# The convolution's output product in seven products instead of eight, with weight sums made by accumulating transfers

## The chip, the core and the metric

The kernel runs on one core of a Trainium2 chip. The metric is the device time of one execution in microseconds (us). The engines are PE (matrix products), DVE (elementwise, also called VectorE), ACT (activations and copies), POOL (here almost only the issuing of transfers, among them those that add to their destination) and SP (the issuing of transfers). Each engine takes its instructions in the order in which they were recorded; semaphores order the engines among each other.

## The reference

The model is a trunk of two layers in float32 on 1024 positions of width 1024: a gated short convolution, a SwiGLU FFN, dilated attention, a second FFN, with an RMSNorm before each and one at the end. What the change touches is the convolution mixer and the norm behind it:

```
def short_conv_mixer(h, w_in, conv_k, w_out):
    b, c, u = jnp.split(h @ w_in, 3, axis=-1)
    y = depthwise_causal_conv(c * u, conv_k)     # width 3
    return (b * y) @ w_out
...
h = rms_norm(x, mix_norm[0]);  x = x + short_conv_mixer(h, ...)
h = rms_norm(x, ffn_norm[0]);  x = x + (silu(h @ w_gate) * (h @ w_up)) @ w_down
```

## The kernel before

Everything is held transposed: `X[n]` is a page of 128 channels by 1024 positions, n = 0 to 7, and the positions are worked on in two halves of 512. Float32 products are made of three matmuls: each operand is split into a high part (a copy on ACT, rounded to the matmul's format) and a low part (a subtraction on DVE), and hi·hi, hi·lo and lo·hi are summed in a PSUM bank. So each weight tile costs one ACT and one DVE instruction (`split`, L157 and L158), and so does each operand tile (`hi`, L604 and L605).

Most large products use a seven-product scheme for 2 by 2 blocks (class `Strassen`): weights in rows and contraction halves, activations in contraction halves and position halves. The seven products are numbered 1 to 7; 3, 5, 6 and 7 take sums of weight blocks and sums of activation blocks. Sums of weights are made on DVE (`combo`, L225). The sums of activations for an FFN's down product are made when a quad of blocks is complete (`store`, L784), and go to DRAM as `part`; `feed` brings them back (`hin`), splits them and hands them to `down`, which runs the products in the order of `DOWN`: 1, 2, 6, 7, 4, 5, 3.

The convolution's output product was the exception. `Conv.store` put each block y to DRAM as `plain_conv`; `first_tiles` and `group1` multiplied whole tiles: first channels 0 to 3 for all eight n and both halves (`first_tiles`, added to a loaded X), then channels 4 to 7, the first position half for all n, and then the second half (`by_columns`, called by `group1`). After each addition into X, `chained` squares it (ACT) for the next norm and POOL or DVE adds the squares; at the end of the first half the statistics are summed over channels by PE with a matrix of ones, and `first_half` makes the FFN's first operands one by one: `scaled` (DVE, tile hcol), its high part (ACT), then the previous one's low part (DVE). `gained` follows on ACT for each n whose second half is complete.

The order on each engine is the order in which this Python code records; there is no planner. `ensure` and `take` decide how far ahead weights are split. `bias_tables` makes the attention's bias tables in three pieces, placed at three points of the first FFN's down product by `after`.

## Time and profile before

| | us |
|---|---|
| median of 3 runs | 2089.16 (2088.01 to 2090.88) |
| profiled execution | 2087.8 |
| its span, first to last instruction | 2086.0 |
| PE busy | 2069.0 (99%) |
| DVE busy | 1760.0 (84%) |
| ACT busy | 1027.9 (49%) |
| POOL busy | 269.8 (13%) |

The convolution's input products run until 242.2 us, its output product from 242.22 to 329.76, where the FFN's first product begins. The profile's page gives a matmul's busy time from start to modelled end; in the order of time one sees when each starts. Idle time of an engine is put down to what ended it.

### The profile page before, as it was taken

How to read it: one execution, taken by the hardware profiler on the slowest of the kernel's cores; microseconds unless marked ns; L12 is line 12 of the kernel's file. 1: busy time of each engine (PE TensorE's matmuls, PEld its weight loads, DVE VectorE, ACT ScalarE, POOL GpSimd, SP SyncE). 2: the span in 40 equal slices, each digit the busy share in tenths (PEclk: the TensorE clock that was granted, in tenths of full speed). 3: DMA queues.
4: the chain of work that ended last, by engine and by line, in shares of the span. 5: the costliest groups of instructions: out<-in, count | busy, mean ns of one | idle time of the engine just before them, and what ended most of it. 6: DMA issues, size and time to landing. Idle time of an engine off the chain costs nothing.

```text
span 2086.0 us, 30813 instructions
## 1 busy us (share of the span) xinstructions
PE 2069.0 (99%) x10954; PEld 1784.5 (86%) x10954; DVE 1760.0 (84%) x3302; ACT 1027.9 (49%) x1902; POOL 269.8 (13%) x381
## 2 busy tenths in 40 slices
PE   9999999999999999999999999999999999999998
PEld 7788888888888888878889999998888888888887
DVE  8898769988888889798985888987998888887896
ACT  8333427444444455355544666665544444455443
POOL 1000000110100111010223333211001011002000
PEclk9999999999999999999999999999999999999999
DMA  7332643233233477443657867855222333368532
GB/s 222 96 96 71 237 131 76 102 106 111 102 107 101 159 247 209 161 127 128 227 187 207 210 173 219 240 186 143 76 91 101 106 107 106 115 204 228 162 101 81
DMA packets 133929, 305.70 MB, mean 147 GB/s; under 512 B 15580, under 2 KB 46382, under 8 KB 133776
## 3 DMA queue, kind: packets, MB, share of 16 engines
q1 hardware_dynamic: 96128, 203.51, 32.2%
q0 software_dynamic: 30016, 85.52, 13.5%
q10 hardware_dynamic: 7632, 14.70, 1.9%
q8 instruction: 87, 1.43, 0.3%
q14 instruction: 66, 0.54, 0.1%
HBM read 209.99 MB, written 84.50 MB: 141 GB/s over the span
## 4 chain that ended last, share of the span: by engine, by line
PE 94%; DVE 3%; ACT 1%; issue 0%; DMA 0%; DVEq 0%; ACTq 0%
PE bank L612 21%; PE bank L614 21%; PE bank L613 21%; PE bank L1714 5%; PE bank L415 3%; PE bank L416 3%; PE bank L417 3%; PE bank L707 3%; PE bank L704 3%; PE bank L706 3%; PE bank L1583 2%; PE bank L1585 1%; PE bank L1584 1%; PE bank L1640 1%; PE bank L1639 1%; DVE b L605 0%
## 5 line engine op out<-in xcount | busy, mean ns | idle before, releaser
L612 PE MATMUL bank<-b,w 128*128 128x512 f32 x2064 | 804.4, 390 | 3.0 <-ACT w L157 1.6
L614 PE MATMUL bank<-b,w 128*128 128x512 f32 x2064 | 804.0, 390 | 3.1 <-DVE w L158 3.0
L613 PE MATMUL bank<-b,w 128*128 128x512 f32 x2064 | 804.1, 390 | 0.6 <-DVE b L924 0.6
L614 PEld LDWEIGHTS bank<-b,w 128*128 128x128 f32 x2064 | 387.5, 188 | 86.9 <-DVE w L158 6.1
L612 PEld LDWEIGHTS bank<-b,w 128*128 128x128 f32 x2064 | 387.7, 188 | 83.1 <-ACT w L157 2.0
L613 PEld LDWEIGHTS bank<-b,w 128*128 128x128 f32 x2064 | 387.7, 188 | 79.7 <-DVE b L924 1.4
L157 ACT ACTIVATE w<-combo 128x512 fp32r<-128x512 f32 (+2 forms) x496 | 259.0, 549 | 266.7 <-DVE combo L225 227.9
L158 DVE TENSOR_TENSOR w<-combo,w 128x512 fp32r<-128x512 f32 (+2 forms) x496 | 286.2, 590 | 33.0 <-ACT w L157 32.7
L618 ACT ACTIVATE part<-bank 128x512 f32<-128x512 f32 x192 | 114.4, 596 | 394.0 <-PE bank L614 390.6
L158 DVE TENSOR_TENSOR w<-raw,w 128x512 fp32r<-128x512 f32 (+2 forms) x340 | 190.4, 581 | 36.8 <-ACT w L157 36.6
L622 DVE TENSOR_TENSOR part<-part,bank 128x256 f32<-128x256 f32 (+1 forms) x372 | 174.8, 498 | 34.8 <-PE bank L614 18.6
L157 ACT ACTIVATE w<-raw 128x512 fp32r<-128x512 f32 (+2 forms) x340 | 171.3, 537 | 27.4 <-PE bank L707 10.5
L415 PE MATMUL bank<-w_hi,w 128*128 128x512 f32 (+1 forms) x336 | 126.3, 376 | 0.0
L416 PE MATMUL bank<-w_lo,w 128*128 128x512 f32 (+1 forms) x336 | 124.2, 370 | 0.0
L417 PE MATMUL bank<-w_hi,w 128*128 128x512 f32 (+1 forms) x336 | 124.2, 370 | 0.0
L839 DVE TENSOR_TENSOR x<-x,bank 128x512 f32<-128x512 f32 x136 | 92.8, 683 | 30.0 <-PE bank L614 29.1
L225 DVE TENSOR_TENSOR combo<-raw 128x512 f32<-128x512 f32 (+1 forms) x176 | 116.0, 659 | 0.0
L605 DVE TENSOR_TENSOR b<-hin,b 128x512 fp32r<-128x512 f32 x140 | 95.2, 685 | 15.6 <-ACT b L604 15.5
L534 DVE TENSOR_TENSOR x<-x,bank 128x512 f32<-128x512 f32 (+1 forms) x88 | 55.7, 635 | 41.3 <-PE bank L417 40.6
L604 ACT ACTIVATE b<-hin 128x512 fp32r<-128x512 f32 x140 | 86.0, 619 | 5.1 <-DMA hin<-part 3.6
L707 PE MATMUL bank<-b,w 128*128 128x256 f32 x288 | 81.5, 283 | 0.0
L706 PE MATMUL bank<-b,w 128*128 128x256 f32 x288 | 81.5, 283 | 0.0
(233 smaller groups left out, 3318.5 us busy)
## 6 DMA issues: line engine op xcount, KB each, us to landing
hin<-part SPq DMA_DIRECT2D x140, 256.0 KB, 4.4
raw<-in_ffn_w_gate SPq DMA_DIRECT2D x44, 512.0 KB, 3.6
raw<-in_ffn_w_up SPq DMA_DIRECT2D x44, 512.0 KB, 3.6
part<-sum POOLq DMA_DIRECT2D x80, 256.0 KB, 2.3
raw<-in_attn_w_qkv SPq DMA_DIRECT2D x27, 512.0 KB, 4.5
raw<-in_conv_w_in SPq DMA_DIRECT2D x24, 512.0 KB, 4.2
raw<-in_ffn_w_down SPq DMA_DIRECT2D x32, 384.0 KB, 5.3
part<-part POOLq DMA_DIRECT2D x40, 256.0 KB, 2.5
```

The costliest lines, as they stand in the source:

```text
L157: nc.scalar.activation(hi, src, AF.Copy)
L158: low = lambda: eng.tensor_tensor(out=lo, in0=src, in1=hi, op=ALU.subtract)
L225: eng.tensor_tensor(out=c, in0=a, in1=b, op=op)
L415: nc.tensor.matmul(b, whi[:, a], ahi[:, s], start=first, stop=False)
L416: nc.tensor.matmul(b, whi[:, a], alo[:, s], start=False, stop=False)
L417: nc.tensor.matmul(b, wlo[:, a], ahi[:, s], start=False, stop=last)
L612: nc.tensor.matmul(b, hi[:, a], bhi, start=start and k == 0, stop=False, skip_group_check=True)
L613: nc.tensor.matmul(b, hi[:, a], blo, start=False, stop=False, skip_group_check=True)
L614: nc.tensor.matmul(b, lo[:, a], bhi, start=False, stop=k == n - 1, skip_group_check=True)
L622: nc.vector.tensor_tensor(out=t, in0=t, in1=b, op=ALU.add)
L706: nc.tensor.matmul(b, hi[:, a], blo, start=False, stop=False, skip_group_check=True)
L707: nc.tensor.matmul(b, lo[:, a], bhi, start=False, stop=k == n - 1, skip_group_check=True)
```

## The change

The output product joins the seven-product scheme (`CONV_PAIRS, CONV_CHUNK = 4, 4`: all eight channel tiles in one chunk of four pairs). `first_tiles`, `halved` and `below` go; `down` serves the convolution too, with four units of two n each for the seven products. `store` makes four differences for each of the four quads, and signs are chosen such that the weights are only added: the banks of odd n hold the negated result and are subtracted from X[n] instead of added.

- `add_summed` replaces DVE's sums of weights: two pages for each unit, a and b, are loaded; after a block has been split, an accumulating transfer on POOL adds the next weight block to it in the page. The FFN's weights keep DVE's sums (`add_pair`), with the sign turned.
- `ensure` loads these pages ahead by `LEAD = 4` weights. The conv's operands are read one tile ahead (`feed(1)`), the first four during the last unit's products 7, 4 and 3 (`CONV_FEED`).
- X starts with ACT's copy of a bank; the source is added by an accumulating transfer on POOL (after products 1, 6 and 7), or loaded by SP and added to.
- `entry` replaces `group1` ahead of the first FFN: squares, spills and the first half's operands follow products 2, 4, 5 and 3. The first half of the even n is complete with product 2, of the odd n with product 4, the second half with products 5 and 3. `first_half` makes the odd tiles 1, 3, 5, 7 first and then 0, 2, 4, 6, each together with `gained`.
- `bias_tables` runs later, at three points of the down product's last chunk: (0,7,2), (0,4,4), (0,5,4) instead of (-1,3,2), (0,1,2), (0,2,0).

```diff
+    def add_summed(u, ab, cd, w):
...
+        def part(m):
+            p = t["a" if m in (1, 7, 6, 3) else "b"]
+            left, right = p[:, :w], p[:, w:2 * w]
+            out = split(left if m in (1, 2, 7) else right, None, nc.vector)
+            if m == 1:
+                accumulate(pair(p), twice(cd))
+            elif m == 2:
+                accumulate(t["a"][:, w:2 * w], block(cd, 1))
+            elif m == 6:
+                accumulate(right, block(ab, 1))
+            elif m == 4:
+                accumulate(right, block(cd, 0))
...
         def down(self, c, feed):
...
+                if fresh and not (one and (n % 2, h) == (1, 0)):
+                    nc.scalar.activation(X[n][:, half(h)], b, AF.Copy, scale=-1.0 if n % 2 else 1.0)
                 else:
-                    nc.vector.tensor_tensor(out=X[n][:, half(h)], in0=X[n][:, half(h)], in1=b, op=ALU.add)
+                    nc.vector.tensor_tensor(out=X[n][:, half(h)], in0=X[n][:, half(h)], in1=b,
+                                            op=ALU.subtract if n % 2 else ALU.add)
...
+        def entry(c, m, k):
+
+            j = k // 2
...
+            if m not in (2, 4, 5, 3):
+                return
+            n, h, at = k + (m in (4, 5)), int(m in (5, 3)), j + 4 * (m in (4, 3))
+            norm.chained(at, *HALVES[h], 0, n)
+            nc.scalar.dma_start(spill[n][:, half(h)], X[n][:, half(h)])
...
+            elif (m, j) == (5, 1):
+                run(pre.pop())
+                pre.append(sw.first_half((1, 3, 5, 7, 0, 2, 4, 6)))
+            if m == 3:
+                ensure(first_op + 2 + j)
+            for t in {(5, 2): (1,), (5, 3): (3,), (3, 0): (5, 7), (3, 1): (0,), (3, 2): (2,), (3, 3): (4, 6)}.get((m, j), ()):
+                step(t)
...
-            if (c, m, k) in ((-1, 3, 2), (0, 1, 2), (0, 2, 0)):
+            if (c, m, k) in ((0, 7, 2), (0, 4, 4), (0, 5, 4)):
                 next(tab, None)
```

The change moves much of the order. The first place is DVE at the end of the output product. Before, the FFN's first product takes operands k = 0 to 3, and the last of their low parts (b_2819) stood among additions of the second half; x is a page of X, hcol a normed tile, acc the sum of squares:

```order
L605 TENSOR_TENSOR b_2813<-hcol_2811,b_2813 128x512
L534 TENSOR_TENSOR x_2310<-x_2310,bank_2823 128x512
L1312 SCALAR_TENSOR_TENSOR hcol_2840<-x_2310,gains_68,rstd_2583 128x512
L605 TENSOR_TENSOR b_2819<-hcol_2817,b_2819 128x512
L534 TENSOR_TENSOR x_2345<-x_2345,bank_2847 128x512
```

Two more tiles of the output product followed on PE behind the bank of x_2345. Now k = 2 is the tile of x_2319, and its low part (b_3007) stands behind the addition of the output product's very last bank, 2889; w is a weight's pair of parts:

```order
L160 TENSOR_TENSOR w_3002<-raw_2736,w_3002 128x512
L1336 SCALAR_TENSOR_TENSOR hcol_3005<-x_2319,gains_68,rstd_2422 128x512
L649 TENSOR_TENSOR b_2980<-hcol_2978,b_2980 128x512
L896 TENSOR_TENSOR x_2388<-x_2388,bank_2889 128x512
L533 TENSOR_TENSOR acc_2421<-acc_2421,sq_2997 128x512
L160 TENSOR_TENSOR w_3028<-raw_2736,w_3028 128x512
L1336 SCALAR_TENSOR_TENSOR hcol_3031<-x_2349,gains_68,rstd_2422 128x512
L649 TENSOR_TENSOR b_3007<-hcol_3005,b_3007 128x512
```

The low part has moved from a place well ahead of the first product to one behind the last addition. The second place is POOL around the last quad. Before, its queue held the stores alone:

```order
L771 DMA plain_conv_6_165<-y_1883 128x512
L771 DMA plain_conv_7_166<-y_2105 128x512
L771 DMA plain_conv_7_166<-y_2048 128x512
L771 DMA plain_conv_6_165<-y_2185 128x512
L492 DMA acc_2582<-sq_2591 128x512
```

Now accumulations into the weight pages (summed) and into X stand between them; part_conv_3_2 is the last quad's tile for product 2:

```order
L843 DMA part_conv_3_1_180<-y_2028 128x512
L235 DMA summed_2075<-in_conv_w_out 128x2x512
L235 DMA summed_2096<-in_conv_w_out 128x2x512
L843 DMA part_conv_3_3_182<-y_2182 128x512
L235 DMA summed_2123<-in_conv_w_out 128x2x512
L235 DMA summed_2147<-in_conv_w_out 128x2x512
L235 DMA summed_2075<-in_conv_w_out 128x512
L886 DMA x_2286<-in_x 128x512
L235 DMA summed_2096<-in_conv_w_out 128x512
L886 DMA x_2319<-in_x 128x512
L843 DMA part_conv_3_2_181<-y_2120 128x512
```

The second transfer into summed_2096 follows the first into the same page, and the store of part_conv_3_2 has come to stand behind both.

More of the change, by code (lines that the diff above doesn't have):

```diff
@@ L216, in add_slab, with accumulate, load, add_pair @@
         ops.append((key, lambda: split(get_raw(i)[:, :width(src)])))
-    def add_pair(u, rows, w, eng, upto, low=()):
+    def add_summed(u, ab, cd, w):
+        t = {}
+        block = lambda src, h: view(src, h * w, [[1, w]])
+        twice = lambda src: view(src, 0, [[0, 2], [1, w]])
+        pair = lambda p: view(p, 0, [[w, 2], [1, w]])
+        rows = (cd.offset - ab.offset, 2)
+        def accumulate(dst, src):
+            nc.gpsimd.dma_start(out=dst, in_=src, accum_op=ALU.add)
+        def load(name):
+            t[name] = page("summed")
+            nc.sync.dma_start(pair(t[name]), twice(ab) if name == "a" else view(ab, w, [rows, [1, w]]))
+        def part(m):
[10 more added lines that the diff above has]
+                accumulate(right, block(cd, 0))
+            if m in (5, 3):
+                del t["a" if m == 3 else "b"]
+            return out
+        fetch_of["m", u, 1], fetch_of["m", u, 2] = lambda: load("a"), lambda: load("b")
+        return {m: (("m", u, m), lambda m=m: part(m)) for m in WINOGRAD}
+    def add_pair(u, rows, w, eng, upto, low=(), sub=ALU.subtract):
         t = {}
@@ L593, in __init__ @@
             self.st, self.quads, self.hid, self.deep = {}, {}, {}, {}
-            self.banks = set()
+            self.banks, self.there, self.after = set(), set(), None
+            self.lead = 1 if key == CONV else 2
             self.ahead, self.now = 2, 0
@@ L852, in down, with drain @@
                     add(n, h, b)
-                    if c == 0 and m in (2, 4, 5, 3):
-                        nc.gpsimd.dma_start(out=X[n][:, half(h)], in_=self.source[n][:, half(h)], accum_op=ALU.add)
+                    if c == 0 and m in ((1, 6, 7) if one else (2, 4, 5, 3)):
+                        source(n, h, nc.gpsimd, accum_op=ALU.add)
+                    if one and m == 1:
+                        X[n + 1] = page("x")
+                        source(n + 1, 0, nc.sync)
                     if m == 4:
                         del p[k]
+                    self.drain(c, m, k)
                     if k // 2 in steps:
                         next(feed, None)
-                    self.downed(c, m, k)
-        def downed(self, c, m, k):
+                    if self.after:
+                        self.after(c + 1 - len(self.chunks), m, k)
+        def drain(self, c, m, k):
             pass
@@ L889, in filled @@
                 if self.key == CONV:
-                    self.below(n, last)
+                    if self.order[n] in CONV_FEED:
+                        for _ in range(CONV_FEED[self.order[n]]):
+                            next(feed)
                 else:
@@ L1009, in conv @@
                     nc.vector.scalar_tensor_tensor(o, a, tap(i), o, op0=ALU.mult, op1=ALU.add)
-            eng = nc.vector
-            eng.tensor_tensor(out=y, in0=y, in1=self.norm.rstd[:, half(h)], op=ALU.mult)
+            nc.vector.tensor_tensor(out=y, in0=y, in1=self.norm.rstd[:, half(h)], op=ALU.mult)
             self.y[t, h] = y
@@ L1051, in idle, with drain, mix @@
                 self.step(2)
-        def halved(self, fs):
-            raw = {}
-            for f in list(fs) + [None]:
-                if f is not None:
-                    raw[f] = page("hin")
-                    nc.sync.dma_start(raw[f], self.plain[f])
-                for g in list(raw):
-                    if g != f:
-                        self.hid[g] = split(raw.pop(g))
-                yield
-        def below(self, n, last):
-            if self.order[n][0] == last and n >= self.at(last, 2) - self.base:
-                ensure(self.base + n + 2)
-                next(self.low, None)
-            if self.order[n] == (last, 7):
-                self.load_x(0, 1)
-                ensure(self.at(last, 3) + 2)
-        def first_tiles(self):
-            run(self.low)
-            upper = self.halved(range(CO, KT))
-            for n in range(KT):
-                banks = two_banks()
-                run(product(take(("co", 0, n), min(max(n - 2, 2), 4)), range(CO), self.hid, banks))
-                if n + 2 < KT:
-                    self.load_x(n + 2)
-                add_to_x(n, banks)
-                self.step(4 if n < 2 else None)
-                if n >= 3:
-                    next(upper, None)
-            run(upper)
-            for f in range(CO):
-                del self.plain[f]
+        def drain(self, c, m, k):
+            if self.waiting:
+                self.step(4 if (m, k) in ((1, 0), (1, 2)) else None)
         def out(self, u, c, v):
             self.waiting.append(self.work(u, c, v))
-        def mix(self, group1):
-            norm = self.norm
+        def mix(self, entry):
+            norm, self.after = self.norm, entry
             prep = self.operands()
@@ L1315, in scaled, with first_half @@
             return t
[L1317 removed]
+        def first_half(self, order=range(KT)):
             lo = None
[L1319 removed]
+            for k in order:
                 t = self.scaled(k, 0, half_page("hcol"))
```

121 lines of the change are left out of this document (69 added, 52 removed).

## The prediction

> **What bounds the kernel now.** I read the page first, then PE's waits, then the stage that is rewritten. The page says that one engine sets the time:
>
> ```profile
> span 2086.0 us, 30813 instructions
> PE 2069.0 (99%) x10954; PEld 1784.5 (86%) x10954; DVE 1760.0 (84%) x3302; ACT 1027.9 (49%) x1902; POOL 269.8 (13%) x381
> ```
>
> PE is busy for 2069.0 of 2086.0 us, so a matmul taken out is worth its time unless a new wait takes its place. PE's time per matmul must not be read from the page's mean of 390 ns: that is a matmul from start to modelled end, and successive ones overlap. The order of time of the convolution's output product shows the pitch:
>
> ```profile
> 242.22 0.39 PE L415 MATMUL bank<-w_hi,w 128*128 128x512 f32 x1
> ...
> 329.54 0.39 PE L417 MATMUL bank<-w_hi,w 128*128 128x512 f32 x1
> 329.76 0.39 PE L612 MATMUL bank<-b,w 128*128 128x512 f32 x1
> ```
>
> 384 matmuls and 2 small column sums lie between 242.22 and 329.76: 87.54 / 386 = 0.2268 us each. Now the stage by windows (columns: PE, PEld, DVE, ACT and POOL busy with their counts, granted clock, DMA share, GB/s), and the only wait of PE from 242 to 400 us:
>
> ```profile
> 104.00:156.00 52.00, 52.00 (x231) 43.08 (x230) 49.64 (x99) 19.77 (x35) 3.80 (x7) 1.00 0.31 97
> 242.00:286.00 44.00, 44.00 (x196) 36.44 (x195) 27.13 (x44) 11.52 (x17) 1.62 (x3) 1.00 0.53 181
> 317.00:330.00 13.00, 13.00 (x60) 10.74 (x59) 11.13 (x18) 10.34 (x18) 2.56 (x3) 1.00 0.51 114
> 330.00:360.00 30.00, 29.73 (x131) 24.30 (x130) 29.64 (x50) 20.75 (x36) 2.57 (x3) 1.00 0.30 74
> ```
> ```profile
> PE bank L528 <- DVE sum L520: 0.3, 1, 0.3
> ```
>
> The granted clock is 1.00 and PE never stands still, but the stage ends beside a VectorE that is almost full: 11.1 of 13 us, then 29.6 of 30. It stays ahead because all additions into the first half of X were done before the second half's products began, so the first half's norm could be worked on under them. That lead is what I look for in the changed order.
>
> **What the change takes off PE.** Seven products of 4 row units by 4 contraction tiles by 3 matmuls are 336 instead of 384: 48 x 0.2268 = **10.9 us**. (By the 0.39 mean it would be 18.7; the rows above exclude that.) The bias table's four matmuls now stand before a later product. Where they stood, the waits of PE over the whole run name two:
>
> ```profile
> PE bank L560 <- issue: 1.1, 1, 1.1
> PE bank L612 <- DVE t L562: 0.8, 1, 0.8
> ```
> ```profile
> 892.40 1.84 DVE L562 TENSOR_TENSOR t<-bank,low 16x512 f32<-16x512 f32 x4
> ```
>
> The first is the fourth of these matmuls, which finds no free bank because DVE is behind with its additions; the second is the product after them, which waits for DVE to read a bank. At the new place DVE has fewer additions before it, so I take off 1.9 us (bounds 0 and 1.9). Their vector work (the third row begins it) now ends nearer to query/key's first products; I add back a third of its 1.84, 0.6 (bounds 0 and 1.9).
>
> The conv stage gains four differences for each of four quads, 2.4 us of DVE and four stores on POOL a quad. Two of the quads fall about the fullest window, 104:156: DVE busy for 49.6 us there in 99 instructions, but each of them overlaps the next by 0.085 (0.685 from start to end, 0.60 from start to start, below), so some 41 of 52 us are taken, and 4.8 more fit. I cost these at nothing until the last quad; without that cover they would cost 4.8.
>
> **The seam into the FFN, on DVE and ACT.** Durations for it come from the old seam. First DVE, then ACT, in order of time:
>
> ```profile
> 316.18 0.75 DVE L1312 SCALAR_TENSOR_TENSOR hcol<-x,gains,rstd 128x512 f32<-128x512 f32 x1 [1.94 <-ACT rstd L530]
> 316.85 0.68 DVE L534 TENSOR_TENSOR x<-x,bank 128x512 f32<-128x512 f32 x1
> 318.76 0.69 DVE L158 TENSOR_TENSOR w<-raw,w 128x512 fp32r<-128x512 f32 x1 [1.24 <-ACT w L157]
> 319.37 0.75 DVE L1312 SCALAR_TENSOR_TENSOR hcol<-x,gains,rstd 128x512 f32<-128x512 f32 x1
> ...
> 321.95 0.69 DVE L158 TENSOR_TENSOR w<-raw,w 128x512 fp32r<-128x512 f32 x1 [0.64 <-ACT w L157]
> ...
> 340.99 2.49 DVE L1342 TENSOR_TENSOR x<-x,rstd 128x512 f32<-128x512 f32 x4
> ```
> ```profile
> 317.50 0.71 ACT L1334 ACTIVATE x<-x,less 128x512 f32<-128x512 f32 x1
> 318.12 0.62 ACT L157 ACTIVATE w<-raw 128x512 fp32r<-128x512 f32 x1
> 318.64 0.62 ACT L489 ACTIVATE sq<-x 128x512 f32<-128x512 f32 x1
> ```
>
> Four x<-x,rstd in 2.49 with the last at 0.69 give a DVE pitch of 0.60; hcol's is 0.66 (316.18 to 316.85). On ACT a gain takes 0.62, a copy or square 0.52. The hand-off is the point: hcol starts at 316.18, ACT makes its high part, then the gained X, then a weight's high part, and the weight's low part on DVE starts at 318.76, **2.58 us** after hcol began. DVE fills only what stands between: with one addition between, it idles 1.24; with two (319.37 to 321.95), 0.64.
>
> In the changed order I walk the two queues from the addition that follows product 4's third unit (L896) to the low part of operand k = 2 (L649), for which the FFN's first product waits. On DVE that is 52 instructions; ahead of the last stand 45 of 0.60 and 6 of 0.66, 31.0 us. The waits for ACT in it, each by the chain above less what stands between:
> - w after the first half's statistics: addition 0.72, square 0.52, Ln, Exp and w some 0.6 each, less two instructions of 0.6 between: 1.9 (the row at 316.18 shows 1.94 for the like).
> - w after hcol with nothing between: 2.58 - 0.66 = 1.9; the next with one instruction between: 1.3.
> - w after an addition (0.72), its square (0.52) and w (0.65), with one instruction between: 1.3; three more of this kind with two or more between: 0.75, 0.75, 0.1.
>
> Together 8.0. With 0.4 until the first addition's bank is ready, 0.3 of dependent latency and 0.7 for the last to be ready, the low part is there at 40.4 us. PE has 118 matmuls from the same zero, 26.8 us. So PE stands still for **13.6 us** in all: about 1.0 at the statistics' sums, 2.5 at product 3's fourth operand and 10 inside the FFN's first product, at the operands k = 0 and k = 2. What is late next is covered: the following products ask for less than these waits have already given. Bounds: with no wait for ACT it is 31.0 + 1.4 - 26.8 = 5.6; with each wait as worked out, 13.6. I take 13.6, since the old seam shows these idles at their full size.
>
> **The seam into product 2, on POOL.** The old rows for transfers (count, KB each, median us from issue to landing): the FFN's stores over the whole run; store and read of 225 to 262 us; the accumulating adds of squares over the whole run; the FFN's from 700 to 800 us; and what an accumulating issue takes of POOL (ns):
>
> ```profile
> part<-sum POOLq DMA_DIRECT2D x80, 256.0 KB, 2.3
> ...
> plain_conv<-y POOLq DMA_DIRECT2D x4, 256.0 KB, 3.0
> hin<-plain_conv SPq DMA_DIRECT2D x4, 512.0 KB, 3.3
> acc<-sq POOLq DMA_DIRECT2D x6, 512.0 KB, 5.1
> x<-spill POOLq DMA_DIRECT2D x15, 256.0 KB, 8.8
> part<-sum POOLq DMA_DIRECT2D x8, 256.0 KB, 3.6
> hin<-part SPq DMA_DIRECT2D x39, 256.0 KB, 5.9
> ```
> ```profile
> L854 POOL DMA_DIRECT2D x<-spill x11: 860/862/991, 782.4 to 801.6; - x11
> ```
>
> Product 2's fourth operand comes from the last quad. Its store now stands on POOL behind a second accumulation into a page, which waits until the first (512 KB) has landed. Zero is the start of the last unit's product 4. The weight's low part that frees the page ends at 4.5 us by DVE's list; the first accumulation lands 9.0 later (an estimate from the 8.8 row) at 13.5; two accumulations of 0.86 on POOL, store issued at 15.3; landed 2.4 later (between the old page's 2.3 for the FFN's stores and the 3.0 here), read back 3.3, high part 0.7: 21.7. PE wants it after 81 matmuls, 18.4, and has lost 0.4 by then to a late operand of product 1. So it waits **2.9**, and 0.5 for the low part. Bounds: if the accumulation takes 5.1, DVE's own list rules the store (13.6) and the wait is 1.2; if it takes 10.4 (1.6 more than the 8.8 of half its bytes), the store 3.6 and the read 5.9 us, 8.0. I stay at 2.9, nearest to the rows of this place. The Trainium skill, "DMA: Bandwidth & Descriptors", section "Anatomy of one DMA — SWDGE (gpsimd) path", fits a GpSimd-issued transfer by 2.0 us plus its bytes over 436 GB/s, an estimate of 3.2 us for 512 KB; by it the wait would be the low bound, 1.2, and the time 2092.7. The trace's plain stores (3.0) are near that fit, and its accumulations (8.8 for half the bytes) are not.
>
> The later accumulations have 9 us and more before their weights are split, except product 5's, whose ACT copy comes 9.5 us after the issue: marginal, put into the range.
>
> **Sum.** -10.9 - 1.9 + 0.6 + 0.4 + 2.9 + 0.5 + 13.6 = +5.2 against the profiled execution's 2087.8 us (span 2086.0 and 1.8 around it): 2093.0. The median of the runs shown, 2089.16, is 1.4 above that execution, so I put the time at **2094.4**. About 0.2%, 4.2 us, is what can be told from no change here.
>
> **Rivals.**
> - *The hand-offs are covered* (faster). If ACT's copies of weights are all early, only DVE's list counts at the seam: 5.6 for 13.6, and 1.2 for 2.9. -10.9 - 1.9 + 0.6 + 0.9 + 1.2 + 5.6 = -4.5: 2084.7. For it: ACT is busy for 49%. Against: its copies stand behind squares that wait for DVE, and the old seam idled by just these amounts. It decides as soon as the seven waits come to less than 1. Chance 0.08.
> - *Accumulations are quick*: 1.2 for 2.9, +3.5, 2092.7, which is no change by the bound. The 5.1 row speaks for it, the 8.8 row against it. It decides where a 512 KB accumulation takes under some 6 us. Chance 0.20. The Trainium skill's fit, above, would have it so.
> - *Transfers are crowded at product 2*: 8 pages of weights, 8 tiles of operands, 8 halves of X and 8 accumulations, some 12 MB, move within about 32 us there, 370 GB/s, where the row 242:286 shows 181. The wait becomes 8.0: 2099.5. Chance 0.15.
> - *The bias move does nothing*: the two waits go along to the new place; +1.9, 2096.3. Against it: the two waits hang on DVE's place at the moment, which differs. Chance 0.10.
>
> **Chances.** The forecast has 0.47; of it a quarter falls inside 4.2 us (sizes are good to some 2 us), as do the quick accumulations for the most part. Faster 0.07, within 0.2% 0.29, slower 0.64. The range takes in the quick and the crowded case: 2089 to 2099.5.
>
> **What would show it.** Right: PE waits named L657 <- DVE b L649 of 2 to 4 us, three or so, and L656 <- ACT b of 3 to 4 where the FFN's first product begins; DVE idle at w L160 <- ACT w L159 of 1.3 to 1.9, four times; L656 <- ACT b near the output product's second group; no L603 or L605 in PE's list. PE's instruction count falls by 48. Wrong: PE busy through that seam with only DVE saturated; then the hand-off arithmetic fails. A wait of PE for a weight after an accumulation would mean that the transfers, not DVE, set the stage.

## The result

The changed kernel takes **2117.1 us** (2111.6 to 2122.0 in four executions) against 2088.6 for the one before: ratio 1.0134, 95% interval 1.0107 to 1.0161. Four more executions later gave 2111.7 (2111.6 to 2116.9), ratio 1.0119 (1.0106 to 1.0132): four of the eight lie at 2111.6 to 2111.8, the rest 4 to 10 us above. The profiled execution is one of the shorter, 2111.6. The forecast was 2094.4 with an upper end of 2099.5: slower, as forecast, but by five times as much.

The page after, and two places that both kernels pass, the FFN's first gate and query/key's first high part (duration min/median/max, then first and last start), before and after:

```profile
span 2109.2 us, 30920 instructions
PE 2070.2 (98%) x10906; PEld 1780.5 (84%) x10906; DVE 1774.8 (84%) x3334; ACT 1049.3 (50%) x1946; POOL 302.3 (14%) x421
```
```profile
L1386 ACT ACTIVATE gate<-bank x4: 580/582/597, 366.4 to 1511.2; 128x512 f32<-128x512 f32 x4
L1207 ACT ACTIVATE kq_hi<-kq x28: 624/633/638, 1002.1 to 1110.2; 128x512 fp32r<-128x512 f32 x28
```
```profile
L1410 ACT ACTIVATE gate<-bank x4: 577/590/600, 390.3 to 1534.4; 128x512 f32<-128x512 f32 x4
L1231 ACT ACTIVATE kq_hi<-kq x28: 622/633/637, 1024.9 to 1132.9; 128x512 fp32r<-128x512 f32 x28
```

PE runs 48 matmuls fewer, as worked out, and yet its first gate comes 23.9 us later, at 390.3. From there on the two kernels run alike: 22.8 behind at query/key, 23.2 at the end. So all of the loss lies in the rewritten stage, before 390 us, and the bias table took about 1 us of it back. The stage by windows (columns as in the prediction), then PE in order of time at the four places where it stands:

```profile
245.00:262.00 17.00, 11.16 (x47) 8.66 (x47) 10.91 (x21) 5.64 (x11) 10.73 (x15) 0.92 1.12 221
262.00:282.00 20.00, 14.09 (x51) 11.20 (x52) 9.10 (x14) 7.84 (x14) 5.74 (x7) 0.73 1.01 299
302.00:322.00 20.00, 15.80 (x61) 11.78 (x60) 12.27 (x20) 8.55 (x15) 1.13 (x2) 0.88 0.89 239
342.00:362.00 20.00, 12.52 (x46) 9.06 (x45) 18.55 (x30) 13.99 (x24) 3.44 (x4) 0.83 0.42 92
```
```profile
255.77 0.40 PE L658 MATMUL bank<-b,w 128*128 128x512 f32 x1
267.91 0.79 PE L656 MATMUL bank<-b,w 128*128 128x512 f32 x1 [11.74 <-ACT b L648]
268.63 0.79 PE L657 MATMUL bank<-b,w 128*128 128x512 f32 x1
269.22 0.63 PE L658 MATMUL bank<-b,w 128*128 128x512 f32 x1
269.65 0.63 PE L656 MATMUL bank<-b,w 128*128 128x512 f32 x1
...
272.64 0.51 PE L657 MATMUL bank<-b,w 128*128 128x512 f32 x1
272.99 0.39 PE L658 MATMUL bank<-b,w 128*128 128x512 f32 x1
...
318.43 0.80 PE L656 MATMUL bank<-b,w 128*128 128x512 f32 x1 [2.62 <-ACT b L648]
319.83 0.79 PE L657 MATMUL bank<-b,w 128*128 128x512 f32 x1 [0.61 <-DVE b L649]
...
348.15 0.79 PE L656 MATMUL bank<-b,w 128*128 128x512 f32 x1 [3.70 <-ACT b L648]
351.88 0.80 PE L657 MATMUL bank<-b,w 128*128 128x512 f32 x1 [2.94 <-DVE b L649]
...
355.65 0.50 PE L657 MATMUL bank<-b,w 128*128 128x512 f32 x1 [0.84 <-DVE b L649]
```

Two losses are to be read here. The waits in brackets, 25.4 us in all from 242 to 362 us: 0.3 in product 1, 11.7 at product 2's fourth operand, 4.1 as product 5 begins (0.90, 2.62, 0.61), 1.8 at product 3's fourth operand (0.86, 0.90), 7.5 in the FFN's first product. And what comes after them: from 269.22 to 272.64 matmuls start every 0.43 us instead of 0.2268, and the granted clock of that window is 0.73. Taking each start from the next, less 0.2268 and less the wait, from 242 to 362 us, these slow matmuls cost another 9.9 us; the same count gives 0.3 for the kernel before. -10.9 - 1.9 + 25.4 + 9.9 = +22.5 of the 23.2.

The Trainium skill, "TensorE: Matmul & The Clock Gate", section "What's actually happening", has the array fall to half its clock after an idle window of about 3.4 us and return after a busy one. Behind the long wait the trace agrees: half the rate (0.43), from 267.91 to 272.99. At product 5 shorter waits were enough: 2.62 and 0.61, with a single matmul between them.

Why the operand was late is told by its way, the end of the result y on DVE, its store on POOL, the read on SP, the high part on ACT, and by the transfers of those 17 us (GB/s in 40 slices; packets, MB and share of the 16 engines' time of POOL's queue, q0; then count, KB each, median us to landing):

```profile
250.36 0.68 DVE L1092 TENSOR_TENSOR y<-y,part 128x512 f32<-128x512 f32 x1
...
251.43 1.24 POOL L843 DMA_DIRECT2D part_conv<-y  x1
...
261.43 0.33 SPq L865 DMA_DIRECT2D hin<-part_conv  x1
...
267.22 0.63 ACT L648 ACTIVATE b<-hin 128x512 fp32r<-128x512 f32 x1 [12.66 <-DMA hin<-part_conv]
```
```profile
GB/s 202 202 207 212 207 212 202 222 323 328 246 236 193 202 222 193 202 222 193 207 217 198 198 222 193 202 222 188 207 222 188 207 212 241 352 304 222 207 212 202
DMA packets 1881, 3.76 MB, mean 221 GB/s; under 512 B 176, under 2 KB 176, under 8 KB 1880
...
q0 software_dynamic: 1877, 3.75, 112.1%
...
summed<-in_conv_w_out POOLq DMA_DIRECT2D x2, 512.0 KB, 9.0
summed<-in_conv_w_out POOLq DMA_DIRECT2D x4, 256.0 KB, 9.0
x<-in_x POOLq DMA_DIRECT2D x4, 256.0 KB, 9.7
part_conv<-sum POOLq DMA_DIRECT2D x4, 256.0 KB, 7.7
part_conv<-y POOLq DMA_DIRECT2D x1, 256.0 KB, 9.9
```

POOL did not send the store out late: y ends at 251.04 and the store goes out at 251.43, earlier than I had worked out. But it landed 9.9 us later, and the read, issued at once, took 5.8 more. The 16 DMA engines were busy the whole time (share 1.12) and moved only some 205 GB/s in most slices, 221 in the mean.

### The profile page after: what moved, and what is told of

It is laid out like the page before. It is cut to its first block, busy times and chain, and to the rows that moved or that the text cites. A ratio compares the mean times of both kernels' runs of the same rounds, so it can differ in the third digit from the quotient of the medians.

```text
span 2109.2 us, 30920 instructions
## 1 busy us (share of the span) xinstructions
PE 2070.2 (98%) x10906; PEld 1780.5 (84%) x10906; DVE 1774.8 (84%) x3334; ACT 1049.3 (50%) x1946; POOL 302.3 (14%) x421
## 4 chain that ended last, share of the span: by engine, by line
PE 91%; DMA 3%; DVE 3%; ACT 1%; issue 1%; POOL 0%; SPq 0%; DVEq 0%; ACTq 0%; POOLq 0%
PE bank L658 21%; PE bank L656 21%; PE bank L657 21%; PE bank L1761 5%; PE bank L748 3%; PE bank L751 3%; PE bank L750 3%; PE bank L458 2%; PE bank L460 2%; PE bank L459 2%; PE bank L1630 1%; PE bank L1632 1%; PE bank L1631 1%; PE bank L1687 1%; PE bank L1686 1%
## 5 line engine op out<-in xcount | busy, mean ns | idle before, releaser
L656 PE MATMUL bank<-b,w 128*128 128x512 f32 x2176 | 852.2, 392 | 20.9 <-ACT b L648 18.9
L657 PE MATMUL bank<-b,w 128*128 128x512 f32 x2176 | 851.5, 391 | 6.8 <-DVE b L649 6.5
L658 PE MATMUL bank<-b,w 128*128 128x512 f32 x2176 | 849.8, 391 | 2.0 <-DVE w L160 1.9
L656 PEld LDWEIGHTS bank<-b,w 128*128 128x128 f32 x2176 | 410.5, 189 | 108.2 <-ACT b L648 21.5
L657 PEld LDWEIGHTS bank<-b,w 128*128 128x128 f32 x2176 | 410.3, 189 | 95.0 <-DVE b L649 10.1
L658 PEld LDWEIGHTS bank<-b,w 128*128 128x128 f32 x2176 | 410.3, 189 | 89.5 <-DVE w L160 4.4
L160 DVE TENSOR_TENSOR w<-raw,w 128x512 fp32r<-128x512 f32 (+2 forms) x324 | 180.2, 577 | 37.9 <-ACT w L159 37.8
L159 ACT ACTIVATE w<-raw 128x512 fp32r<-128x512 f32 (+2 forms) x324 | 162.0, 532 | 15.3 <-PE bank L751 10.2
L649 DVE TENSOR_TENSOR b<-hin,b 128x512 fp32r<-128x512 f32 x168 | 114.4, 685 | 40.1 <-ACT b L648 40.0
L896 DVE TENSOR_TENSOR x<-x,bank 128x512 f32<-128x512 f32 x152 | 103.8, 683 | 32.0 <-PE bank L658 30.8
L648 ACT ACTIVATE b<-hin 128x512 fp32r<-128x512 f32 x168 | 103.3, 619 | 24.0 <-DMA hin<-part_conv 15.6
L751 PE MATMUL bank<-b,w 128*128 128x256 f32 x288 | 81.5, 283 | 0.0
L750 PE MATMUL bank<-b,w 128*128 128x256 f32 x288 | 81.5, 283 | 0.0
L748 PE MATMUL bank<-b,w 128*128 128x256 f32 x288 | 81.3, 282 | 0.0
L458 PE MATMUL bank<-w_hi,w 128*128 128x512 f32 (+1 forms) x208 | 76.4, 368 | 0.0
L459 PE MATMUL bank<-w_lo,w 128*128 128x512 f32 (+1 forms) x208 | 74.4, 357 | 0.0
L460 PE MATMUL bank<-w_hi,w 128*128 128x512 f32 (+1 forms) x208 | 74.4, 357 | 0.0
```

What stands on the lines that cost most here:

```text
L159: nc.scalar.activation(hi, src, AF.Copy)
L160: low = lambda: eng.tensor_tensor(out=lo, in0=src, in1=hi, op=ALU.subtract)
L458: nc.tensor.matmul(b, whi[:, a], ahi[:, s], start=first, stop=False)
L459: nc.tensor.matmul(b, whi[:, a], alo[:, s], start=False, stop=False)
L460: nc.tensor.matmul(b, wlo[:, a], ahi[:, s], start=False, stop=last)
L656: nc.tensor.matmul(b, hi[:, a], bhi, start=start and k == 0, stop=False, skip_group_check=True)
```

## Experiments

Medians in us. Each ratio is taken against the kernel before as timed beside that run. Waits and slow matmuls are PE's, of one profiled execution each, 242 to 362 us, by the method above.

| run | time | ratio to before (95%) | waits | slow |
|---|---|---|---|---|
| changed kernel | 2117.1; 2111.7 | 1.0134 (1.0107-1.0161); 1.0119 (1.0106-1.0132) | 25.4 | 9.9 |
| e1_plain | 2102.7 | 1.0065 (1.0050-1.0080) | 14.9 | 10.8 |
| e2_put_act | 2114.1 | 1.0115 (1.010-1.013) | 22.8 | 12.6 |
| e3_no_weight_sums | 2100.3 | 1.0054 (1.0037-1.0070) | 13.8 | 10.6 |
| e4_direct | 2110.5 | 1.0101 (1.0085-1.0118) | 22.4 | 12.7 |
| e5_seam | 2109.3 | 1.0097 (1.0083-1.0111) | 21.4 | 11.0 |
| e6_x_plain | 2119.4 | 1.0132 (1.0116-1.0149) | 26.2 | 10.7 |
| e7_dve_sums | 2101.6 | 1.0058 (1.0044-1.0072) | 14.9 | 11.2 |
| e8_before_late_bias | 2086.5 | 0.9989 (0.9980-0.9998) | 0.3 | 0.3 |
| e9_busy | 2112.9 | 1.0114 (1.0099-1.0130) | 16.3 | 9.8 |
| best2 | 2094.7 | 1.0033 (1.0023-1.0043) | 10.6 | 7.7 |
| best3 | 2094.8 | 1.0035 (1.0021-1.0048) | 12.1 | 6.4 |
| best5 | 2096.0 | 1.0043 (1.0029-1.0056) | 10.1 | 7.2 |
| low_two | 2112.6 | 1.0112 (1.0096-1.0127) | 25.7 | 11.4 |
| best6 | 2096.4 | 1.0032 (1.0020-1.0045) | 10.2 | 7.6 |

### Is it accumulating, or the bytes, or the queue?

**e1_plain.**

```
-            nc.gpsimd.dma_start(out=dst, in_=src, accum_op=ALU.add)
+            nc.gpsimd.dma_start(out=dst, in_=src)
...
-                        source(n, h, nc.gpsimd, accum_op=ALU.add)
+                        source(n, h, nc.gpsimd, **({} if one else dict(accum_op=ALU.add)))
```

> The convolution's accumulating transfers (weight sums and source rows of x) become plain copies of the same bytes into the same places, from the same queue, in the same order: the sums are left out, nothing else. After: 2117.1 us, a wait of 11.7 us at product 2's fourth operand, 4.1 us at product 5's first matmuls, 202 to 222 GB/s in 245 to 262 us. Theory 'an accumulating transfer holds the DMA engines about twice as long per byte': the stretch moves near 400 GB/s, the store lands about 4 us after its issue instead of 9.9 and the read 3 instead of 5.3, so the wait falls from 11.7 to about 3.5, product 5's to under 0.5, and with the slow clock behind them 2117.1 - 8.2 - 3.7 - 3 = about 2102. Theory 'it is the bytes, or their place ahead of the store on one queue': the wait stays 10 to 12 and the time 2115 to 2118.

Its transfers of the same window, and the first wait in PE's order of time:

```profile
GB/s 371 424 386 386 424 366 347 299 376 347 347 231 251 212 260 395 386 424 405 424 299 231 231 376 424 376 424 347 342 323 313 333 308 275 337 275 318 275 318 352
DMA packets 1889, 5.75 MB, mean 338 GB/s; under 512 B 308, under 2 KB 308, under 8 KB 1888
...
q0 software_dynamic: 1491, 5.02, 83.7%
...
summed<-in_conv_w_out POOLq DMA_DIRECT2D x4, 256.0 KB, 5.8
x<-in_x POOLq DMA_DIRECT2D x4, 256.0 KB, 5.7
...
part_conv<-y POOLq DMA_DIRECT2D x1, 256.0 KB, 4.7
```
```profile
261.36 0.80 PE L656 MATMUL bank<-b,w 128*128 128x512 f32 x1 [5.59 <-ACT b L648]
```

With nothing changed but the addition in flight (the kernel leaves out these sums), the 17 us move 5.75 MB instead of 3.76, a quarter-MB transfer lands in 5.7 to 5.8 us instead of 9 to 9.7, the store in 4.7 instead of 9.9. A MB of POOL's queue takes 83.7 / 5.02 = 16.7% of the engines' time instead of 112.1 / 3.75 = 29.9%, which is 1.8 times as much with the additions, the plain stores of the queue counted in. The wait is 5.6 instead of 11.7, product 5's are gone, and the time is 2102.7 where 2102 was expected. So 6.1 us of the first wait and all of product 5's belong to accumulating; the other 5.6 remain with plain copies, more than the 3.5 expected.

**e3_no_weight_sums.**

```
         def accumulate(dst, src):
-            nc.gpsimd.dma_start(out=dst, in_=src, accum_op=ALU.add)
+            pass
```

> The sixteen accumulating transfers of the convolution's output weights are left out (products then multiply unsummed blocks); those of x stay. In 242 to 262 us that takes 3.0 of the 4.3 MB of GpSimd's queue away. Theory 'accumulations fill the DMA engines': the store lands in about 5 us, the wait of 11.7 falls to about 4, and product 5's 4.1 us go (nothing to wait for), time 2117.1 - 7.7 - 4.1 - 3 = about 2102. Theory 'the sources of x, or the read back, make the wait': 9 to 12 us remain at product 2, only product 5's go, time 2111 to 2113.

2100.3, with 4.5 us left at product 2 and none at product 5: as the first theory has it. Leaving the sixteen transfers out altogether, with X's accumulations kept, gains only 2.3 us more than making both kinds plain.

**e2_put_act.**

```
-            nc.gpsimd.dma_start(self.parts[q, m], t)
+            eng = nc.scalar if self.key == CONV and q == 3 else nc.gpsimd
+            eng.dma_start(self.parts[q, m], t)
```

> The last quadruple's seven stores go to ScalarE's queue instead of GpSimd's; nothing else. Theory 'the store stands in line behind the accumulations on GpSimd's queue': it lands in 3 to 4 us instead of 9.9, the wait at product 2's fourth operand falls from 11.7 to about 5.5, time about 2110. Theory 'the sixteen DMA engines are full whoever issues': the store still takes 7 to 10 us, the wait stays 9 to 12, time 2114 to 2118.

2114.1, between the two medians of the changed kernel, so the time decides nothing. The stores of the sums landed in 7.8 us from ScalarE's queue, in 7.7 from GpSimd's. The store of y itself, the one that product 2 waits for, was issued at 252.37 and its read went out at 258.72, so it landed in some 6 us instead of 9.9; its read then took 7.0 instead of 5.8. The waits at product 2 came to 8.0 (1.15 at its third operand, 0.23, 6.62 at its fourth) instead of 11.7, between the two theories. GpSimd's queue was a part of that store's delay, then, and the full engines another; how they share it is not shown.

**e6_x_plain.**

```
-                if fresh and not (one and (n % 2, h) == (1, 0)):
+                if fresh and not one:
...
+                    if one and m == 1:
+                        for j in (k, k + 1):
+                            X[j] = page("x")
+                            for h in range(2):
+                                source(j, h, nc.sync)
...
-                    if c == 0 and m in ((1, 6, 7) if one else (2, 4, 5, 3)):
+                    if c == 0 and not one and m in (2, 4, 5, 3):
```

> The rows of x are loaded plainly ahead of product 1, all sixteen halves, and VectorE adds every product to them: the twelve accumulating transfers of x go, ScalarE's twelve copies out of the banks too, VectorE gets twelve adds (0.6 us each, 7 us over 85 us); the weight sums stay accumulating. Theory 'accumulations fill the engines, in proportion to their bytes': 1.0 of the 4.0 MB that accumulate in 238 to 262 us goes, so a quarter to a third of the 11.7 us (3 to 4), and product 5's 4 us, whose weights stood in line with x's rows: 2117.1 - 3.5 - 4 - 2 = about 2107.5. Rival 'plain loads of the same bytes only shift the crowd ahead, and VectorE pays': 2113 to 2120.

No gain: 2119.4. The rival held. Product 5's waits for its operands did go: with X's rows out of GpSimd's queue, its four weight sums landed 6.2 us after their issue (median) instead of 11.7, so it was X's rows that they stood in line with. But product 2's third operand now came late (2.1 us for its high part, 4.7 for the low one) and then its fourth (8.3); that the loads, now all ahead of the weight accumulations, are the cause fits the rival and is not shown apart. Its profiled execution, 2120.9, is moreover one of the longer kind told of below.

### Is it one operand, or the stretch?

**e4_direct.** DIRECT is ((3, 2),), the last quad and product 2; the first piece is in `put`, the second in `feed`.

```
+            if self.key == CONV and (q, m) in DIRECT:
+                self.kept[q, m] = t
+            else:
+                nc.gpsimd.dma_start(self.parts[q, m], t)
...
+                    if (self.chunks[d][j], mm) in self.kept:
+                        raw[n] = self.kept.pop((self.chunks[d][j], mm))
+                        n += 1
+                        continue
```

> Product 2's fourth operand is split straight from the convolution's result in SBUF; its store and its read back are left out, the accumulations stay. The value is there at 251.0 us, ScalarE and VectorE need 1.3 more, TensorE comes at 256.2. Theory 'the round trip through a full DMA system is the 11.7 us': that wait goes with the slow clock behind it, 2117.1 - 11.7 - 2.5 = about 2103, waits of product 5 and of the feed-forward stay. Rival 'the stretch is late as a whole': the wait comes back at product 6's or 7's fourth operand, which are stored and read 5 to 9 us later in the same stretch, with 4 to 8 us; time 2107 to 2112.

The wait that took the place of the one removed:

```profile
276.94 0.80 PE L657 MATMUL bank<-b,w 128*128 128x512 f32 x1 [7.20 <-ACT b L649]
```

At product 2 nothing is waited for but 0.23; at product 6's fourth operand 7.2 are, and the time falls to 2110.5 only, 1 us below the changed kernel's shorter executions. The second theory held: the stretch is late, not the one round trip.

**e7_dve_sums.**

```
-            if i == CONV:
-                units = [add_summed((i, c, 2 * u), src(2 * u), src(2 * u + 1), span) for u in range(4)]
-            else:
+            if True:
                 raw_src.extend(src(2 * u + v) for v in range(2) for u in range(4))
```

> The sums of the convolution's output weights are made by VectorE from plainly loaded blocks (16 sums of 128x512, about 0.61 us each in a row, 9.7 us in all) instead of by accumulating transfers; x keeps its accumulating sources. Theory 'accumulations fill the DMA engines, VectorE has room': the waits are those of the run without weight sums (4.5 us at product 2, none at product 5), plus 0 to 3 us more at the seam into the feed-forward: 2100 to 2104. Rival 'the sums only move the load': TensorE waits for weights from VectorE in products 6, 7, 5 and 3 by 6 to 10 us, time 2107 to 2112.

2101.6, inside the 2100 to 2104 of the first theory, 4.1 us left at product 2, none at product 5, and TensorE waits for no weight. VectorE has room for sixteen sums there; the DMA engines had none for sixteen accumulations.

### The seam into the feed-forward

**e5_seam.**

```
-                pre.append(sw.first_half((1, 3, 5, 7, 0, 2, 4, 6)))
+                pre.append(sw.first_half((0, 1, 2, 3, 5, 7, 4, 6)))
...
+            for _ in range({(5, 2): 2, (5, 3): 2, (3, 0): 2, (3, 1): 1, (3, 2): 1}.get((m, j), 0)):
+                next(pre[0])
             for t in {(5, 2): (1,), (5, 3): (3,), (3, 0): (5, 7), (3, 1): (0,), (3, 2): (2,), (3, 3): (4, 6)}.get((m, j), ()):
-                step(t)
+                sw.gained(t)
```

> The eight scaled halves that the feed-forward's first product multiplies are made in the order 0, 1, 2, 3, 5, 7, 4, 6 instead of 1, 3, 5, 7, 0, 2, 4, 6, four of them during product 5; the scratch halves stay where they are. After showed waits of 0.86 + 0.90 at product 3's fourth operand and 3.70 + 2.94 + 0.84 at the feed-forward's first product, 9.2 us, and some 3.5 us of slow clock behind them. Theory 'the last operands in that order set the seam': the 7.5 us at the first product go with about 2 us of slow clock, 2117.1 - 9.5 = about 2107.5. Rival 'VectorE's list as a whole sets it': the wait moves ahead, to product 3's fourth operand (4 to 7 us instead of 1.8), time 2113 to 2118.

The longest wait left behind product 2, in the feed-forward's first products:

```profile
353.50 0.80 PE L657 MATMUL bank<-b,w 128*128 128x512 f32 x1 [3.17 <-DVE b L649]
```

2109.3 (2108.8 to 2109.7). The 3.70, 2.94 and 0.84 are gone; 3.2 came back at the low part of operand 4, which in this order is made behind operand 6's scaled half, one addition of X later. Product 3's waits stayed (0.80, 0.91). So the first theory held for some 4 of its 7.5 us, and slow matmuls took 1.2 back. Against the shorter executions of the changed kernel 2.3 us are left, in the trace (the first gate at 388.0 instead of 390.3) and in the time.

**best2, best3, best5** put the gains together: VectorE's sums, the last quad's operands of products 2, 6 and 7 kept in SBUF, the new order with the last low part one step earlier. In best2 DIRECT is ((3, 2), (3, 6), (3, 7)) and the numbers of scaled halves end with (3, 3): 1. best3 moves TensorE's two statistics sums one unit later, from (5, 1) to (5, 2), and the scaled halves with them. best5 takes the plain order and issues the scratch half ahead of the scaled ones:

```
-                pre.append(sw.first_half((0, 1, 2, 3, 5, 7, 4, 6)))
+                pre.append(sw.first_half(range(KT)))
...
+            for t in {(5, 3): (1,), (3, 0): (3,), (3, 1): (5, 0), (3, 2): (7, 2), (3, 3): (4, 6)}.get((m, j), ()):
+                sw.gained(t)
+            for _ in range({(5, 2): 2, (5, 3): 2, (3, 0): 2, (3, 1): 2, (3, 2): 1}.get((m, j), 0)):
+                next(pre[0], None)
```

> Weight sums by VectorE; the last quadruple's operands of products 2, 6 and 7 split straight from SBUF; scaled halves in the order 0, 1, 2, 3, 5, 7, 4, 6, the last low part one step earlier. Sum of what the single runs gave: 2101.6 (VectorE's sums) - 4.1 - 2.5 (the wait left at product 2, and the slow clock behind it) - 7.8 (the order) - 1 (the last low part, half of it covered) = about 2086, 2 to 3 us below before. Theory 'the gains add, each wait has its own cause': 2084 to 2088. Rival 'VectorE now carries sums, splits and scaled halves in one list, the waits meet again at product 3's and the first product's operands': 2090 to 2095.

> The same, and TensorE's two sums for the first norm half come one unit later (behind product 5's third unit instead of its second), the scaled halves start one unit later. The run with VectorE's sums showed two waits of 0.9 us each at those two matmuls. Theory 'only the hand-off ScalarE - VectorE - TensorE is waited for there': 1.8 us less than the kernel without this, 2082 to 2086. Rival 'the scaled halves then come too late': the wait comes back at product 3's operands or the feed-forward's first product, 2086 to 2092.

> The kernel with VectorE's weight sums and direct splits of products 2, 6 and 7 once more, with the scaled halves in plain order 0 to 7 and, in each step, ScalarE's scratch half (0.71 us) issued ahead of the scaled halves instead of behind them, so that ScalarE works on it while VectorE scales. There VectorE stood idle 1.1 to 1.25 us five times, until ScalarE's high part of a weight, which stood behind the scratch half. Theory 'hand-offs between ScalarE and VectorE set the rest of the seam': 0.6 us less at each of four or five steps, 2094.7 - 2 to 3 = about 2092. Rival 'VectorE's list is full, so its order moves nothing': 2094 to 2096.

2094.7, 2094.8 and 2096.0: by their medians each missed its first theory, and all stay slower than before. (best5's shorter executions, 2091.4 and 2092.3, do lie where its first theory put them, and best3 lies above the 2086 to 2092 of its rival too.) The waits at product 2 and 6 are down to 1.6 and 0.7. The seam is not: in best2 8.0 us of waits and 4.0 of slow matmuls still stand between 306 and 342 us, in best3 the two sums wait no longer and product 3's operand waits 1.7 + 0.9 and the first product 2.8 + 3.2 instead. In best5 VectorE's idle time at weights did fall from 6.6 to 4.9 us, and the wait went to the statistics sums of the second half (3.3 us). That fits the rival, VectorE's list as a whole: in each of these three orders something else was late. That no order would do is not shown.

### The clock

**e9_busy.**

```
+                    if one and (m, k) == (2, 0):
+                        idle_hi = self.b[1][0][0]
+                        for _ in range(48):
+                            nc.tensor.matmul(b, idle_hi[:, :128], idle_hi, start=True, stop=True, skip_group_check=True)
                     self.mm((c, k), m, b, m in (1, 2, 5), 4)
```

> The changed kernel with 48 extra matmuls into product 2's first bank ahead of its first own matmul (48 x 0.227 = 10.9 us, inside the wait of 11.7); their result is overwritten. Theory 'the granted clock falls because TensorE stood idle': a wait of about 0.8 remains, the matmuls behind it keep a pitch near 0.23 instead of 0.43 to 0.72, the clock of 262 to 282 us is 0.95 or more instead of 0.73, time 2117.1 - 2.5 = 2114.6. Rival 'the clock falls for another reason there': pitch and clock as before, time 2116 to 2118.

Its window (columns as before), and PE's order of time behind the wait:

```profile
262.00:282.00 20.00, 17.35 (x74) 13.53 (x73) 8.51 (x14) 7.87 (x15) 6.46 (x8) 1.00 1.06 310
```
```profile
269.27 0.50 PE L656 MATMUL bank<-b,w 128*128 128x512 f32 x1 [2.37 <-ACT b L648]
270.00 0.50 PE L657 MATMUL bank<-b,w 128*128 128x512 f32 x1 [0.23 <-DVE b L649]
270.33 0.39 PE L658 MATMUL bank<-b,w 128*128 128x512 f32 x1
270.57 0.40 PE L656 MATMUL bank<-b,w 128*128 128x512 f32 x1
```

The granted clock there is 1.00 instead of 0.73 and the pitch 0.24: it is idleness that lowers the clock, as expected. The time, 2112.9, is 1.3 above the shorter executions of the changed kernel, though: the slow matmuls behind the later waits grew by what was saved here (9.8 in all against 9.9). As a cure it was worth nothing that can be told.

### The bias table, and the longer executions

**e8_before_late_bias.**

```
-            if (c, m, k) in ((-1, 3, 2), (0, 1, 2), (0, 2, 0)):
+            if (c, m, k) in ((0, 7, 2), (0, 4, 4), (0, 5, 4)):
```

> The kernel before with nothing but the bias table made at the later places. Forecast term: two waits of TensorE (1.1 and 0.8 us) go, nothing else moves, 2088.6 - 1.9 = 2086.7. Rival 'moving it does nothing': 2088.6. Rival 'it now meets the query and key stage': 2089 to 2090.

All of PE's waits that the view lists for this run:

```profile
PE bank L614 <- DVE w L158: 2.7, 3, 1.6
PE bank L612 <- ACT w L157: 1.8, 2, 1.6
PE bank L1973 <- DVE ones L1967: 1.0, 1, 1.0
PE bank L528 <- DVE sum L520: 0.4, 2, 0.3
```

The 1.1 at L560 and the 0.8 at L612<-DVE t are gone, and nothing has come in their place: 2086.5, where 2086.7 was forecast. Waits of 0.7 and 0.6 at other operands (L923 and L924), which the view lists before, are gone too, so the two waits are not the whole of the difference in the traces. This is the one kernel here that is faster than the one before, by 0.1%.

**after_again, low_two, best6** ask where the longer executions come from.

> The changed kernel as it is, for more executions and a second profile: its four times ran from 2111.6 to 2122.0 and the profiled one was the shortest. Theory 'the accumulating transfers share the DMA engines differently each time': a profiled execution that is longer by d us shows its d in the waits for the operands that come through memory (product 2, 6, product 5's weights), the waits of the seam into the feed-forward (3.7, 2.9, 0.8) stay within 0.3 us. Rival 'something behind 362 us varies': the waits up to 362 us add up to 25.4 +- 1 again, whatever the time.

The second profile, 2111.6 again, has the same waits (26.0) and tells nothing of the longer ones. But three longer executions of other kernels with this bias table were profiled, and each has a wait that the shorter ones lack. ScalarE in best2 (2098.5, where its median is 2094.7), in order of time:

```profile
953.07 0.35 ACT L603 ACTIVATE low<-bank 16x217 f32<-16x217 f32 x1 [4.98 <-DMA acc<-sq]
```

The bias table's fourth low part takes the half page that an accumulating transfer of squares still reads; ScalarE stands 5.0 us, behind it VectorE and the next accumulation, and the query and key norm's sums keep PE 2.1 + 0.9 us. e6_x_plain's profile (2120.9) has the same wait, 5.4 us. low_two and best6 let the four low parts take turns in two half pages:

```
-        t = [page("t0"), page("t1")]
-        for oh, (c0, c1) in zip(ohs, cols):
+        t, lows2 = [page("t0"), page("t1")], [half_page("low") for _ in range(2)]
+        for j, (oh, (c0, c1)) in enumerate(zip(ohs, cols)):
...
-            b, low = bank(), half_page("low")
+            b, low = bank(), lows2[j % 2]
```

> The changed kernel; the bias table's four low parts take turns in two half pages instead of four, so the fourth one no longer waits for the half page that an accumulating transfer of squares reads. In two longer profiles (2098.5 and 2120.9, other kernels with this bias table) ScalarE stood 4.98 us before that low part, VectorE and GpSimd behind it, and the query and key norm's sums kept TensorE 2 to 3 us more; in the shorter profiles the half page was free in time. Theory 'that wait is the 5 us between the shorter and the longer executions': all executions within 2111 to 2114, median about 2112. Rival 'the crowd at product 2 scatters': 2111.5 to 2122 again, median 2112 to 2118.

> The kernel of the run best5 (2091.4 to 2102.0, median 2096.0), with the same two half pages for the bias table's low parts. By the theory of low_two: the shorter executions alone, 2091.4 to 2094.3, median about 2092, still slower than before by some 4 us (waits of 10.1 us and slow matmuls of 7 stand against 10.9 + 1.9). Rival: 2091 to 2102 again, median 2094 to 2096.

low_two ran from 2110.4 to 2114.8, a little wider than the 2111 to 2114 of its theory and narrower than the changed kernel's 2111.6 to 2122.0, but that is four executions against eight. best6 still scatters, 2093.1 to 2098.4, so its expectation failed; its profile, one of the longer, shows that the wait only moved on to the table's next half page:

```profile
953.15 0.21 DVE L611 TENSOR_TENSOR d<-t 16x64 f32<-16x64 f32 x1 [2.74 <-DMA acc<-sq]
```

That the bias table, where it now stands, takes pages that accumulations hold, and that PE then waits some 3 us at the query and key norm's sums (2.1 + 0.9 in best2 and best6, 2.1 + 0.7 in e6_x_plain), is shown. That this is the whole difference between shorter and longer executions, and that the changed kernel's own longer ones are of this kind, is likely and not shown, since no longer execution of the changed kernel was profiled.

## Why the prediction was right or wrong

**Right: what is taken off PE.** x10906 against x10954 is 48 matmuls; outside the waits the pitch is 0.23. **The bias table** was worth 1.9 by the forecast; in e8_before_late_bias it is 2.4 by the medians (0.4 to 4.2 by the interval) and 1.7 between the two profiled spans. The rival that the move does nothing is out, and the 0.6 added back at query/key is not seen there. That the 1.1 was a missing bank is a guess: its row names no releaser. What the forecast did not see is that at the new place the table takes half pages which accumulations still read.

**Wrong: "The seam into product 2".** The term 2.9 + 0.5 measured 11.7, and 2.8 of slow matmuls behind it: 14.5, an error of 11.1. The failed step is "landed 2.4 later ... read back 3.3". Up to there the list held: the store was issued at 251.43, near my low bound. But I took the durations of the store and the read from rows in which the DMA engines had room. Here the store took 9.9 and the read 5.8, while accumulations kept all engines busy at some 1.8 times the time per MB (112.1% for 3.75 MB against 83.7% for 5.02). Even my upper bound, 8.0, kept those two at 3.6 and 5.9. With plain copies the wait was 5.6, so of the error at this wait (8.3 us) about 2.2 are the crowd of bytes and 6.1 the accumulating. The rival "Transfers are crowded at product 2" had the place and the kind right; it counted bytes as if each cost the same. The Trainium skill's fit for a GpSimd-issued transfer ("DMA: Bandwidth & Descriptors", section "Anatomy of one DMA — SWDGE (gpsimd) path"), by which 3.2 us was the estimate for 512 KB, is far off for these accumulations: 9.0.

**Wrong: "The later accumulations have 9 us and more".** Product 5's weights, called marginal at 9.5 us and costed at nothing, were late: their sums landed 11.7 us after the issue (median). ScalarE stood for them, and the operand that PE waited 2.62 us for stood behind them on ScalarE:

```profile
312.46 0.63 ACT L159 ACTIVATE w<-summed 128x512 fp32r<-128x512 f32 x1 [4.27 <-DMA summed<-in_conv_w_out]
317.23 0.63 ACT L159 ACTIVATE w<-summed 128x512 fp32r<-128x512 f32 x1 [2.15 <-DMA summed<-in_conv_w_out]
317.76 0.61 ACT L648 ACTIVATE b<-hin 128x512 fp32r<-128x512 f32 x1
```

VectorE's waits for ScalarE's high parts over the same instructions, of the changed kernel (300 to 350 us) and then of e1_plain (299 to 340 us; total, count, longest):

```profile
DVE w L160 <- ACT w L159: 13.5, 8, 4.4
```
```profile
DVE w L160 <- ACT w L159: 7.4, 6, 1.9
```

The late weights put 13.5 - 7.4 = 6.1 us into VectorE's list.

**Right: the seam into the FFN, 13.6.** The seven hand-off waits were worked out as 8.0; in e1_plain, where no weight is late, there are six, of 7.4. From product 5's start to the last wait in the FFN's first product PE lost 9.0 us of waits and 5.0 of slow matmuls in e1_plain, together 14.0; in the changed kernel 13.4 and 6.4, together 19.8, against 13.6 + 6.1 = 19.7 with the late weights. I count the slow matmuls in because PE would have waited for the same list anyway; that is an argument, and no run takes them out alone. The parts were less good: 1.8 at product 3's operand instead of 2.5, 7.5 in the first product instead of 10, and none at the statistics' sums.

**Missing: the clock.** The forecast had no term for it. Behind product 2's wait it cost 2.8 us; behind the seam's last wait it cost some 0.5 in this profile of the changed kernel and some 2.8 in e1_plain, where about 13 matmuls were slow.

Of the rest of the error, 2111.6 less 2093.0 being 18.6, the two wrong terms are 11.1 + 6.1 = 17.2. The median on record, 2117.1, lies 5.5 above that execution where I had put 1.4; the likeliest cause is the half page above, and it is not shown.

"What would show it" named the decisive sign, a wait of PE for a weight after an accumulation; it came in a milder form, as VectorE and ScalarE waiting for summed weights.

## What to carry to other kernels

An accumulating transfer saves an engine's instruction and charges the DMA engines more for each byte (here 1.8 times): price it by the rate of accumulating rows (here some 205 GB/s), and price every store and read in its stretch by rows from a stretch that is as full. When seven products replace eight in a short stage, the matmuls saved (10.9 us) must be held against the latency from the last operand to the first product that needs it, since the stage has no other work to put between. A stall of some 3 us should be written down with up to 3 us of half-speed matmuls behind it, unless PE will only wait again.

## What was not expected of the hardware

- With accumulating transfers in the queue the core moved 188 to 222 GB/s in most slices (mean 221) with all 16 engines busy, with plain ones in the same place up to 424 (mean 338). The Trainium skill, "Collectives: The Full Stack", section "The bandwidth ceiling: the fold count and why AG ≠ RS ≠ AR", says of collectives over rings that the add of a ReduceScatter needs two source reads for each byte delivered, which puts it at about half of an AllGather. For sums into SBUF this trace comes near it, with 1.8 times the engines' time for each MB.
- Waits of 2.6 + 0.6 us, or 3.7 + 2.9, already brought the half pitch of 0.43 us, for some 6 to 13 matmuls. How many it is changes: behind the last wait in the feed-forward's first product (0.84) about 2 matmuls were slow in one profile of the changed kernel and 13 in the other.
